# A lower part made by an adding transfer in the second product of an MLP

## The chip, the cores and the metric

The kernel runs on one core of a Trainium2 chip, as one program. The metric is the device time of one execution in microseconds; the number given for a kernel is the median of its runs. A core has five engines that run side by side: TensorE (PE in the profile, its weight loads PEld), VectorE (DVE), ScalarE (ACT), GpSimd (POOL) and SyncE (SP), and 16 DMA engines that move data between HBM and the on-chip memory. Instructions of one engine start in the order in which they stand in its queue, and engines wait for each other on semaphores.

## The reference

A trunk of two layers over 256 tokens of width 2048, in float32. Layer 0 mixes tokens with a convolution module, layer 1 with multi-head latent attention. After each mixer stands an MLP with a squared ReLU, of width 8192, and at the end a norm:

```python
def sq_relu_mlp(h, w1, w2):
    return jnp.square(jax.nn.relu(h @ w1)) @ w2

for layer in range(DEPTH):
    h = rms_norm(x, norm_mixer_g[layer])
    x = x + (conv_module(h, ...) if layer % 2 == 0 else mla(h, ...))
    h = rms_norm(x, norm_mlp_g[layer])
    x = x + sq_relu_mlp(h, mlp_w1[layer], mlp_w2[layer])
return rms_norm(x, final_norm_g)
```

## The kernel before

Every float32 product is made of three matmuls on a reduced-precision type: each operand is split into an upper part `hi` (a copy to that type) and a lower part `lo` (what is left), and `mm3` adds upper by upper, lower by upper and upper by lower into one PSUM bank. The weights come from HBM as they are and are split on the chip. `load` fills a tile `raw` of 1 MB (three of them), with a transfer on SP's queue; `split_half` makes from each half of it a `hi` on ACT (line 159) and a `lo` on DVE (line 160). `hi` and `lo` tiles have six buffers each (`WB`), 128 partitions by 1024 columns.

An MLP is done in two halves of its 8192 hidden columns (`HALVES`). In each half, `mlp` first makes the hidden activations (lines 514 and 515) and splits them into `gh`, `gl` or, for a third of them, into seven combined blocks `sh`, `sl`. Then `down` multiplies them by the second weight matrix. It goes over two column blocks of 1024 output columns (`n2`), and in each over 16 pairs of 128 rows of the weights (`NPAIR`). So there are 2 layers x 2 halves x 2 blocks = 8 passes over 16 pairs.

Pairs 0, 3, 6, 9 and 12 are done with seven block products in place of eight (`seven`): DVE adds weight blocks into a tile `T` (lines 449, 453 and 455), `split_part` splits the blocks and their sums into four `hi` and four `lo` tiles (lines 389 and 390), and PE makes 7 x 3 = 21 matmuls. After pair 12, `early` takes the four banks that are complete and adds their combinations to the residual `xs`: copies on ACT (lines 431 and 432), two subtractions on DVE (433 and 434), two on POOL (437 and 438), and additions to `xs` on DVE (line 555).

The other 11 pairs of a pass are ordinary: two `hi` and two `lo` tiles, and 2 x 2 x 2 x 3 = 24 matmuls (two token tiles `t`, two column blocks of 512, two halves `k`) by `plain`. In the very last pass (layer 1, second half, second block; `last`), pairs 13, 14 and 15 are kept, and their matmuls are done output by output at the end, so that the final norm of each token tile can begin early.

In the MLP no order is written out by hand: a scheduler places the instructions of each engine from the order of the program, its dependences and its own costs. In the convolution and the attention the order is that of the program.

Of the kernel before, what the change touches and what calls it, by code (L numbers as in the profile page):

```python
# [10 lines left out]
F32 = mybir.dt.float32  # L11
F32R = mybir.dt.float32r
BF16 = mybir.dt.bfloat16
I32 = mybir.dt.int32
AF = mybir.ActivationFunctionType
ALU = mybir.AluOpType
AX = mybir.AxisListType

P = 128
D = 2048  # L20
KC = D // P
T = 2
S = T * P
FF = 4 * D
NB = 512
# [16 lines left out]
WB = 6  # L42
# [34 lines left out]
def trunk_kernel(  # L77
# [26 lines left out]
    nc = tc.nc  # L104
# [4 lines left out]
    wpool = ctx.enter_context(tc.tile_pool(name="wpool", bufs=2))  # L109
# [23 lines left out]
    def nm(s):  # L133
        uid[0] += 1
        return f"{s}_{uid[0]}"


    def acc_tile():
        return psum["acc"].tile([P, NB], F32, tag="acc", name=nm("acc"))
# [4 lines left out]
    def load(srcs, nj):  # L144

        raw = wpool.tile([P, nj, sum(src.shape[-1] for src in srcs)], F32, tag="raw", name=nm("raw"), bufs=3)
        at = 0
        for src in srcs:
            nc.sync.dma_start(raw[:, :, at : at + src.shape[-1]], src)
            at += src.shape[-1]  # L150
        return raw

    def split_half(raw, h, eng):

        _, nj, cols = raw.shape
        js = slice(h * nj // 2, (h + 1) * nj // 2)
        hi = wpool.tile([P, nj // 2, cols], F32R, tag="hi", name=nm("hi"), bufs=WB)
        lo = wpool.tile([P, nj // 2, cols], F32R, tag="lo", name=nm("lo"), bufs=WB)
        nc.scalar.activation(hi, raw[:, js, :], AF.Copy)  # L159
        eng.tensor_tensor(lo, raw[:, js, :], hi.bitcast(F32), op=ALU.subtract)  # L160
        return hi, lo

    def split(raw, eng):
# [13 lines left out]
    def rows(w, k0, nk, c0, n):  # L177

        return w[k0 * P : (k0 + nk) * P, c0 : c0 + n].rearrange(
            "(j p) n -> p j n", p=P  # L180
        )

    def mm3(ps, sh, sl, mh, ml, start, stop):

        nc.tensor.matmul(ps, sh, mh, start=start, stop=False)  # L185
        nc.tensor.matmul(ps, sl, mh, start=False, stop=False)  # L186
        nc.tensor.matmul(ps, sh, ml, start=False, stop=stop)  # L187
# [196 lines left out]
    def split_part(src, eng):  # L384

        _, nj, cols = src.shape
        hi = wpool.tile([P, nj, cols], F32R, tag="hi", name=nm("hi"), bufs=WB)
        lo = wpool.tile([P, nj, cols], F32R, tag="lo", name=nm("lo"), bufs=WB)
        nc.scalar.activation(hi, src, AF.Copy)  # L389
        eng.tensor_tensor(lo, src, hi.bitcast(F32), op=ALU.subtract)  # L390
        return hi, lo

    NPAIR = FF // P // HALVES // 2
# [12 lines left out]
    def down(w, k_lo, hs, xs_add, prepare, pre, mp, finish=None, before=None):  # L406

        for n2 in range(NNB // 2):
            na, nb = 2 * n2, 2 * n2 + 1
            banks, seen = {}, set()  # L410
            outs = {(1, nb): "P2", (1, na): "Q3", (0, nb): "P4", (0, na): "Q0"}

            def mm(name, sh, sl, mh, ml, stop):
                if name not in banks:
                    banks[name] = acc_tile()
                mm3(banks[name], sh, sl, mh, ml, name not in seen, stop)
                seen.add(name)

            def plain(p, parts, n, t):
                for k in range(2):  # L420
                    wh, wl = parts[k]
                    gh, gl = (a[:, k, t * P : (t + 1) * P] for a in hs[p])
                    bs = slice((n - na) * NB, (n - na + 1) * NB)
                    mm(outs[t, n], gh, gl, wh[:, 0, bs], wl[:, 0, bs], p == NPAIR - 1 and k == 1)

            def early():

                s1, s5 = (mp.tile([P, NB], F32, tag="v", name=nm("v"), bufs=2) for _ in range(2))
                uv = mp.tile([P, 2, NB], F32, tag="W", name=nm("W"), bufs=1)
                u, v = uv[:, 0, :], uv[:, 1, :]  # L430
                nc.scalar.activation(s1, banks["P1"], AF.Copy)
                nc.scalar.activation(s5, banks["Q5"], AF.Copy)
                nc.vector.tensor_tensor(u, s1, banks["Q6"], op=ALU.subtract)
                nc.vector.tensor_tensor(v, u, banks["Q7"], op=ALU.subtract)
                xs_add(nb, s1, 1)
                xs_add(nb, v, 0)
                nc.gpsimd.tensor_tensor(u, s5, u, op=ALU.subtract)
                nc.gpsimd.tensor_tensor(v, s5, v, op=ALU.subtract)
                xs_add(na, u, 1)
                xs_add(na, v, 0)  # L440

            last = finish is not None and n2 == NNB // 2 - 1
            kept = []
            for p in range(NPAIR):
                raw = load([rows(w, k_lo + 2 * p, 2, na * NB, 2 * NB)], 2)
                if seven(p):
                    x = raw.rearrange("p j (b n) -> p (j b) n", b=2)
                    tt = mp.tile([P, 4, NB], F32, tag="T", name=nm("T"), bufs=1)
                    nc.vector.tensor_tensor(  # L449
                        tt[:, 0:2, :], x[:, 0:1, :].broadcast_to([P, 2, NB]), x[:, 1:3, :], op=ALU.add  # L450
                    )
                    one = split_part(x[:, 1:2, :], nc.vector)
                    nc.vector.tensor_tensor(tt[:, 2, :], tt[:, 0, :], x[:, 2, :], op=ALU.add)
                    t13 = split_part(tt[:, 0:2, :], nc.vector)
                    nc.vector.tensor_tensor(tt[:, 3, :], tt[:, 2, :], x[:, 3, :], op=ALU.add)
                    t24 = split_part(tt[:, 2:4, :], nc.vector)
                    two = split_part(x[:, 2:4, :], nc.vector)
                    gh, gl = hs[p]
                    for name, f, part, i in (
                        ("P1", A11, one, 0), ("Q5", S1, t13, 0), ("Q7", S3, t13, 1), ("Q6", S2, t24, 0),  # L460
                        ("P4", A22, t24, 1), ("P2", A12, two, 1), ("Q3", S4, two, 0),
                    ):
                        mm(name, gh[:, f, :], gl[:, f, :], part[0][:, i, :], part[1][:, i, :],
                           p == LAST_SEVEN and name in ("P1", "Q5", "Q6", "Q7"))
                    if p == LAST_SEVEN:
                        early()
                else:
                    parts = [split_half(raw, h, nc.vector) for h in range(2)]
                    if last and p > LAST_SEVEN:
                        kept.append((p, parts))  # L470
                    else:
                        for t in range(T):
                            for n in (na, nb):
                                plain(p, parts, n, t)
                    if p > LAST_SEVEN and pre:
                        prepare(pre.pop(0))
            if last:
                before()
                for t in range(T):
                    for n in (nb, na):  # L480
                        for p, parts in kept:
                            plain(p, parts, n, t)
                        xs_add(n, banks[outs[t, n]], t)
                        prepare(n, t)
                    finish(t)
            else:
                for t, n in ((0, nb), (1, nb), (1, na), (0, na)):
                    xs_add(n, banks[outs[t, n]], t)
                pre += [na, nb]
        if finish is None:  # L490
            while pre:
                prepare(pre.pop(0))
# [74 lines left out]
    with ExitStack() as cx:  # L567
# [14 lines left out]
        sh = cv.tile([P, KC, S], F32R, name="sh")  # L582
# [203 lines left out]
        with tc.manual_schedule():  # L786
# [6 lines left out]
            for h in range(2):  # L793
                hs = slice(h * D // 2, (h + 1) * D // 2)
# [49 lines left out]
            for c in range(1, KC + 1):  # L844
                n = UC * c
# [84 lines left out]
            for m in range(NP):  # L930
# [4 lines left out]
                for j in range(2):  # L935
                    k = 2 * m + j
                    wh, wl = conv_w(NU + m, j)
                    for b in range(2):
                        bs = slice(b * NB, (b + 1) * NB)
# [7 lines left out]
                t, i = divmod(m, NNB)  # L947
                sl = slice(i * NB, (i + 1) * NB)
# [67 lines left out]
    with ExitStack() as cx:  # L1016
        at = cx.enter_context(tc.tile_pool(name="at", bufs=1, reuse_waits="tile"))
# [56 lines left out]
        raws, parts = {}, {}  # L1074
# [263 lines left out]
        with tc.manual_schedule():  # L1338
# [8 lines left out]
            ps = [[acc_tile() for _ in range(2)] for _ in range(T)]  # L1347
            for k in range(KC):
                u, j = divmod(k, 2)
# [4 lines left out]
                wh, wl = w_at(("kv", u), j)  # L1354
# [9 lines left out]
            ps = [acc_tile() for _ in range(T)]  # L1364
            for k in range(KC):
                u, j = divmod(k, 4)
# [3 lines left out]
                wh, wl = w_at(("q", u), j)  # L1370
# [55 lines left out]
            for g in range(NG):  # L1426
                for i in range(HG):
                    h = g * HG + i

                    n = -(-len(work) // (HG - i))  # L1430
# [116 lines left out]
```

## Time and profile before

| | us |
|---|---|
| median of 3 runs (lowest to highest) | 1974.55 (1972.83 to 1974.62) |
| the profiled execution | 1974.39 |
| its span, first to last instruction | 1972.6 |
| DMA queue of SP: 363.63 MB | 58.1% of 16 engines |

The page names a group of instructions by its line in the kernel, its engine, and the tiles that it writes and reads (`lo<-raw,hi`). "L160 DVE" is so the subtraction of `split_half` on DVE. A timeline row has the start and the length in us, then the engine, line and operation, and in brackets the idle time of the engine before it with what ended it. The length of a matmul is modelled and overlaps the next one, so the pace of PE is read from the distance of the starts. A windows row gives for a stretch its length, the busy time of PE, PEld, DVE, ACT and POOL with the number of their instructions, the granted clock of PE, the busy share of the DMA engines and GB/s.

### The profile page before, as it was taken

The page shows a single profiled execution, that of the slowest core. Times are in us where ns is not written, and L with a number is a line of the kernel's source. Part 1 is how long each engine was busy: PE and PEld are TensorE (multiplying, and loading weights), DVE is VectorE, ACT ScalarE, POOL GpSimd, SP SyncE. Part 2 cuts the span into 40 slices and gives each one's busy share as a digit, 9 for nine tenths or more (in the row PEclk, how much of TensorE's full clock was granted, in tenths as well). Part 3 has the DMA queues.
Part 4 walks back from the last instruction along what each step waited for, and adds up shares of the span by engine and source line. Part 5 has one row for each costly group of instructions (what it writes and reads, how often), then busy time and mean ns, then how long its engine had stood idle before and what let it go on. Part 6 is the DMA issues. An engine that isn't in the chain of part 4 may idle for free.

```text
span 1972.6 us, 28263 instructions
## 1 busy us (share of the span) xinstructions
PE 1945.4 (99%) x10940; PEld 1708.3 (87%) x10940; DVE 1410.4 (71%) x2043; ACT 1032.7 (52%) x1481; POOL 311.0 (16%) x260
## 2 busy tenths in 40 slices
PE   7999999999999999999999999999999999999997
PEld 7999888888888888888899998888888888888886
DVE  5999866666787766678776666566677776667786
ACT  5456655444544444455466665544454444445453
POOL 5999300010000101000001310010100001010000
PEclk9999999999999999999999999999999999999999
DMA  8666456655656665565655445566556676565563
GB/s 241 179 185 186 135 192 186 188 188 168 204 198 203 220 188 188 168 206 195 207 168 179 121 150 178 183 187 188 189 178 200 200 226 188 187 189 199 198 203 117
DMA packets 210502, 367.60 MB, mean 186 GB/s; under 512 B 15416, under 2 KB 89792, under 8 KB 210112
## 3 DMA queue, kind: packets, MB, share of 16 engines
q1 hardware_dynamic: 209344, 363.63, 58.1%
q10 hardware_dynamic: 1024, 2.17, 0.3%
q8 instruction: 85, 1.39, 0.3%
q14 instruction: 49, 0.40, 0.1%
HBM read 363.68 MB, written 2.10 MB: 185 GB/s over the span
## 4 chain that ended last, share of the span: by engine, by line
PE 89%; DVE 8%; ACT 1%; DMA 1%; issue 0%; POOL 0%; POOLq 0%; DVEq 0%; ACTq 0%
PE acc L514 24%; PE acc L187 15%; PE acc L186 15%; PE acc L185 15%; PE acc L515 12%; DVE sum L721 6%; PE acc L620 1%; PE acc L621 1%; PE acc L619 1%; PE acc L241 1%; DVE lo L160 1%; PE sum L669 0%; ACT hi L159 0%; PE acc L1317 0%; DMA xs<-in_x 0%
## 5 line engine op out<-in xcount | busy, mean ns | idle before, releaser
L160 DVE TENSOR_TENSOR lo<-raw,hi 128x1024 fp32r<-128x1024 f32 (+1 forms) x550 | 651.4, 1207 | 367.7 <-ACT hi L159 360.9
L159 ACT ACTIVATE hi<-raw 128x1024 fp32r<-128x1024 f32 (+2 forms) x616 | 622.5, 1040 | 432.4 <-PE acc L514 227.4
L514 PE MATMUL acc<-xt,hi 128*128 128x512 f32 x2048 | 710.5, 390 | 0.0
L515 PE MATMUL acc<-xt,lo 128*128 128x256 f32 x2048 | 578.4, 282 | 0.0
L514 PEld LDWEIGHTS acc<-xt,hi 128*128 128x128 f32 x2048 | 384.4, 188 | 79.7
L515 PEld LDWEIGHTS acc<-xt,lo 128*128 128x128 f32 x2048 | 388.0, 189 | 0.1
L187 PE MATMUL acc<-lo,gh 128*128 128x512 f32 x704 | 274.9, 391 | 2.0 <-DVE lo L160 2.0
L185 PE MATMUL acc<-hi,gh 128*128 128x512 f32 x704 | 274.8, 390 | 0.0
L186 PE MATMUL acc<-hi,gl 128*128 128x512 f32 x704 | 274.7, 390 | 0.0
L389 ACT ACTIVATE hi<-T 128x1024 fp32r<-128x1024 f32 x80 | 84.9, 1062 | 161.9 <-DVE T L449 72.6
L721 DVE SCALAR_TENSOR_TENSOR sum<-ub,w_dw,sum 128x256 f32<-128x256 f32 x400 | 163.7, 503 | 7.1 <-ACT sum L677 6.0
L160 POOL TENSOR_TENSOR lo<-raw,hi 128x1024 fp32r<-128x1024 f32 x66 | 157.5, 2407 | 23.9 <-ACT hi L159 23.9
L529 POOL TENSOR_TENSOR W<-W 128x256 f32<-128x256 f32 x20 | 31.9, 1598 | 819.9 <-DVE W L525 693.9
L185 PE MATMUL acc<-hi,sh 128*128 128x512 f32 x408 | 159.6, 391 | 0.0
L187 PE MATMUL acc<-lo,sh 128*128 128x512 f32 x408 | 159.0, 390 | 0.0
L187 PEld LDWEIGHTS acc<-lo,gh 128*128 128x128 f32 x704 | 132.8, 189 | 30.0 <-DVE lo L160 2.5
L186 PEld LDWEIGHTS acc<-hi,gl 128*128 128x128 f32 x704 | 132.5, 188 | 27.7
L185 PEld LDWEIGHTS acc<-hi,gh 128*128 128x128 f32 x704 | 132.5, 188 | 27.2
L619 PE MATMUL acc<-xt,hi 128*128 128x256 f32 x512 | 144.6, 282 | 0.0
L620 PE MATMUL acc<-xt,hi 128*128 128x256 f32 x512 | 143.2, 280 | 0.5 <-DVE xt L198 0.5
L621 PE MATMUL acc<-xt,lo 128*128 128x256 f32 x512 | 143.2, 280 | 0.3 <-POOL lo L160 0.3
L390 DVE TENSOR_TENSOR lo<-T,hi 128x1024 fp32r<-128x1024 f32 x80 | 97.9, 1225 | 51.6 <-ACT hi L389 51.3
(264 smaller groups left out, 2655.3 us busy)
## 6 DMA issues: line engine op xcount, KB each, us to landing
raw<-in_mlp_w SPq DMA_DIRECT2D x256, 1024.0 KB, 5.5
raw<-in_conv_w_pw SPq DMA_DIRECT2D x64, 512.0 KB, 5.1
raw<-in_conv_w_pw SPq DMA_DIRECT2D x16, 1024.0 KB, 5.0
raw<-in_mla_w_o SPq DMA_DIRECT2D x16, 1024.0 KB, 5.5
raw<-in_mla_w_kv_up SPq DMA_DIRECT2D x8, 1024.0 KB, 5.5
raw<-in_mla_w_in SPq DMA_DIRECT2D x8, 576.0 KB, 3.7
raw<-in_mla_w_in SPq DMA_DIRECT2D x4, 1024.0 KB, 7.1
raw<-in_mla_w_q_up SPq DMA_DIRECT2D x16, 256.0 KB, 3.6
```

What stands on the lines that cost most here:

```text
L159: nc.scalar.activation(hi, raw[:, js, :], AF.Copy)
L160: eng.tensor_tensor(lo, raw[:, js, :], hi.bitcast(F32), op=ALU.subtract)
L185: nc.tensor.matmul(ps, sh, mh, start=start, stop=False)
L186: nc.tensor.matmul(ps, sl, mh, start=False, stop=False)
L187: nc.tensor.matmul(ps, sh, ml, start=False, stop=stop)
L390: eng.tensor_tensor(lo, src, hi.bitcast(F32), op=ALU.subtract)
L514: nc.tensor.matmul(ps[b], wh[:, bs], xhl(k), start=k == 0, stop=False)
L515: nc.tensor.matmul(ps[b][:, :S], wl[:, bs], xh(k), start=False, stop=k == KC - 1)
L619: nc.tensor.matmul(o, wh[:, bs], xh(k), start=k == 0, stop=False)
L620: nc.tensor.matmul(o, wh[:, bs], xl(k), start=False, stop=False)
L621: nc.tensor.matmul(o, wl[:, bs], xh(k), start=False, stop=k == KC - 1)
L721: nc.vector.scalar_tensor_tensor(out=out, in0=ubs[c][:, w : w + S], scalar=tap(c, w), in1=pcs[c], op0=ALU.mult, op1=ALU.add)
```

## The change

In ordinary pairs the first half is split as before. For the second half, `split_dma` makes the upper part on ACT, then on ACT the negative of the upper part into the `lo` tile, and then issues a transfer on POOL's queue that reads the same weights (512 KB) from HBM a second time and adds them onto the `lo` tile. The subtraction of that half on DVE is gone.

The order of the matmuls in ordinary pairs changes too: `whole` takes for each half first the eight matmuls with the upper part of the weights, then the four with the lower part. The pairs that are kept in the very last pass still go through `plain`.

```diff
+    def split_dma(raw, j, src):
+
+        hi = wpool.tile([P, 1, raw.shape[2]], F32R, tag="hi", name=nm("hi"), bufs=WB)
+        lo = wpool.tile([P, 1, raw.shape[2]], F32R, tag="lo", name=nm("lo"), bufs=WB)
+        nc.scalar.activation(hi, raw[:, j : j + 1, :], AF.Copy)
+        nc.scalar.activation(lo, hi.bitcast(F32), AF.Copy, scale=-1.0)
+        nc.gpsimd.dma_start(lo[:, 0, :], src, accum_op=ALU.add)
+        return hi, lo
...
+            def whole(p, parts):
+
+                at = [(t, n, slice((n - na) * NB, (n - na + 1) * NB)) for t in range(T) for n in (na, nb)]
+                for k in range(2):
+                    wh, wl = parts[k]
+                    gh, gl = ([a[:, k, t * P : (t + 1) * P] for t in range(T)] for a in hs[p])
+                    for t, n, bs in at:
+                        ps = bank(outs[t, n])
+                        nc.tensor.matmul(ps, gh[t], wh[:, 0, bs], start=first(outs[t, n]), stop=False)
+                        nc.tensor.matmul(ps, gl[t], wh[:, 0, bs], start=False, stop=False)
+                    for t, n, bs in at:
+                        stop = p == NPAIR - 1 and k == 1
+                        nc.tensor.matmul(bank(outs[t, n]), gh[t], wl[:, 0, bs], start=False, stop=stop)
...
-                    parts = [split_half(raw, h, nc.vector) for h in range(2)]
+                    parts = [
+                        split_half(raw, 0, nc.vector),
+                        split_dma(raw, 1, w[(k_lo + 2 * p + 1) * P : (k_lo + 2 * p + 2) * P, na * NB : (na + 2) * NB]),
+                    ]
                     if last and p > LAST_SEVEN:
                         kept.append((p, parts))
                     else:
-                        for t in range(T):
-                            for n in (na, nb):
-                                plain(p, parts, n, t)
+                        whole(p, parts)
```

More of the change, by code (lines that the diff above doesn't have):

```diff
@@ L411, in down, with bank, first, mm @@
             outs = {(1, nb): "P2", (1, na): "Q3", (0, nb): "P4", (0, na): "Q0"}
-            def mm(name, sh, sl, mh, ml, stop):
+            def bank(name):
                 if name not in banks:
                     banks[name] = acc_tile()
-                mm3(banks[name], sh, sl, mh, ml, name not in seen, stop)
+                return banks[name]
+            def first(name):
+                new = name not in seen
                 seen.add(name)
+                return new
+            def mm(name, sh, sl, mh, ml, stop):
+                mm3(bank(name), sh, sl, mh, ml, first(name), stop)
             def plain(p, parts, n, t):
```

## The prediction

> **What bounds the kernel now.** I read the page's busy table first, then windows of one period of the second product, then its timeline, then the end.
>
> ```profile
> PE   1945.4 (99%) x10940; PEld 1708.3 (87%) x10940; DVE 1410.4 (71%) x2043; ACT 1032.7 (52%) x1481; POOL 311.0 (16%) x260
> 600.60:616.30 15.70, 15.70 (x71) 13.00 (x70) 11.33 (x12) 7.78 (x9) 0.00 (x0) 1.00 0.61 200
> 616.30:632.00 15.70, 15.70 (x71) 12.99 (x70) 11.22 (x12) 7.67 (x9) 0.00 (x0) 1.00 0.62 205
> ```
>
> The two window rows give, after the stretch: its length, then PE, PEld, DVE, ACT and POOL with their counts, the granted clock, the DMA engines' busy share and GB/s. PE is busy for all of the 15.70 us; DVE for some 11.3, ACT 7.7. In this product PE is the bound and DVE is cover.
>
> How fast PE goes is read from the starts in its timeline:
>
> ```profile
> 614.05 0.39 PE L185 MATMUL acc<-hi,gh 128*128 128x512 f32 x1
> 614.28 0.39 PE L186 MATMUL acc<-hi,gl 128*128 128x512 f32 x1
> ...
> 624.71 0.39 PE L187 MATMUL acc<-lo,gh 128*128 128x512 f32 x1
> 624.93 0.39 PE L185 MATMUL acc<-hi,sh 128*128 128x512 f32 x1
> ...
> 629.69 0.39 PE L185 MATMUL acc<-hi,gh 128*128 128x512 f32 x1
> ```
>
> An ordinary pair reads gh and gl, a seven-product pair sh and sl. One period (two ordinary pairs, one of seven products) is 629.69 - 614.05 = 15.64 us for 24 + 24 + 21 = 69 matmuls: 0.2267 us each, with nothing lost between them. So a pair takes 5.44 us or 4.76 us (21 matmuls, 624.93 to 629.69). There is nothing to win here unless a matmul gets quicker.
>
> The one place with a wait is the very end, the last column block of layer 1, where pairs 13 to 15 are kept and run by output:
>
> ```profile
> 1943.18 0.39 PE L185 MATMUL acc<-hi,gh 128*128 128x512 f32 x1
> 1948.40 0.39 PE L185 MATMUL acc<-hi,gh 128*128 128x512 f32 x1
> 1950.82 0.50 PE L187 MATMUL acc<-lo,gh 128*128 128x512 f32 x1 [2.04 <-DVE lo L160]
> 1953.30 0.63 PE L186 MATMUL acc<-hi,gl 128*128 128x512 f32 x1
> 1944.35 2.13 POOL L437 TENSOR_TENSOR W<-v,W 128x512 f32<-128x512 f32 x1 [79.13 <-DVE W L434]
> 1947.12 1.73 POOL L438 TENSOR_TENSOR W<-v,W 128x512 f32<-128x512 f32 x1 [0.63 <-DVE xs L555]
> 1949.55 2.35 DVE L160 TENSOR_TENSOR lo<-raw,hi 128x1024 fp32r<-128x1024 f32 x2
> 1951.60:1955.10 3.50, 3.50 (x10) 2.70 (x9) 1.05 (x2) 0.72 (x2) 0.00 (x0) 0.51 0.00 0
> ```
>
> Pair 15's lower parts stand on DVE behind residual adds that need POOL's L438. PE loses 1950.82 - 1948.40 - 0.23 = 2.2 us, and then runs 3.5 us at a granted clock of 0.51, which costs 1.7 us more. So 3.9 us are all that the change could return here.
>
> **The change, part by part.** There are 11 ordinary pairs in each of 8 column blocks (2 layers, 2 halves, 2 blocks): 88. The prices:
>
> ```profile
> L160 DVE TENSOR_TENSOR lo<-raw,hi 128x1024 fp32r<-128x1024 f32 x526 | 633.3, 1227 | 358.1 <-ACT hi L159 351.7 <-PE acc L241 5.1
> L159 ACT ACTIVATE hi<-raw 128x1024 fp32r<-128x1024 f32 x592 | 606.7, 1055 | 420.5 <-PE acc L514 227.4 <-issue 92.5 <-PE acc L186 78.9
> 624.27 3.90 ACT L159 ACTIVATE hi<-raw 128x1024 fp32r<-128x1024 f32 x4 [3.43 <-issue]
> 625.37 4.63 DVE L160 TENSOR_TENSOR lo<-raw,hi 128x1024 fp32r<-128x1024 f32 x4 [3.08 <-ACT hi L159]
> q1 hardware_dynamic: 209344, 363.63, 58.1%
> raw<-in_mlp_w SPq DMA_DIRECT2D x256, 1024.0 KB, 5.5
> raw<-in_conv_w_pw SPq DMA_DIRECT2D x64, 512.0 KB, 5.1
> raw<-in_mla_w_q_up SPq DMA_DIRECT2D x16, 128.0 KB, 2.4
> ```
>
> Removed: 88 subtractions on DVE, 88 x 1.227 = 108 us of work, 2.45 us in a period. Off the path: gain 0.
>
> Added: 88 negating copies on ACT, 88 x 1.055 = 93 us. ACT goes from 7.7 to 9.8 us of 15.64. They stand between the two upper copies of a pair and what follows on ACT's queue. Price 0, covered by ACT's idle 5.8 us; without that cover 1.055 us a pair.
>
> PE order: still 24 matmuls in a pair, 12 on the half that DVE makes, then 8 uppers of the other, then its 4 lowers. So the late lower part is first read at matmul 20, 20 x 0.2267 = 4.53 us into the pair. Price 0 at an unchanged pace. Freed earlier: the raw half is read by one engine only, and the first half's tiles come free in mid-pair. Both only help the loads.
>
> The new chain: negating copy on ACT, issue on POOL, 512 KB from HBM added onto the tile. The tight case is the pair after a seven-product one. With six hi and six lo buffers, and four of each taken by the seven products, its second lower tile reuses that of the ordinary pair just before them. In the old trace this is seen at 624.27: ACT starts the pair's upper copies when PE is at the end of that pair (624.71), and the pair itself starts at 629.69. In the new order the negating copy may start as soon as that pair's last lower matmul has read the tile, 0.2 us after the pair's end by its 0.39 us, and ends 1.05 us later: 1.3 us. PE needs the sum 4.76 + 4.53 = 9.29 us after the pair's end. **Left for issue and transfer: 8.0 us.** The second ordinary pair reuses the seven products' second tile, which comes free some 2.5 us before they end (after 9 of 21 matmuls); with one upper copy more in its chain its slack is some 2.3 us more.
>
> What issue and transfer cost, no row shows. From below: 2.4 us, the 128 KB load. From above: two 512 KB landings in a row, for reading the old contents and for the load, plus 2.4 us on POOL: 12.6 us. I take 5.1 us for the load and 1.9 us for POOL (its L437 and L438 took 2.13 and 1.73): 7.0 us, nearest to the one row of this size. It fits under 8.0 with 1.0 us to spare, so price 0 in the periods.
>
> POOL's queue: in the blocks' middle only these transfers. At pair 12 the two subtractions of `early` stand between the transfers of pairs 13, 14 and 15. In seven blocks pair 14's sum is needed 10 us after pair 12's end, and a transfer issued at L437's end, 3.3 us after it, lands at 10.3 by my price: 0 to 0.3 us each, 2 us in all at most, taken as 0. In the last block the order by output asks for it much earlier. There the built order puts 22 matmuls before pair 14's late part: needed at 1943.18 + 22 x 0.2267 = 1948.2. It is issued after L437, at 1944.35 + 2.13 = 1946.5, and lands at 1953.5. L438 follows at about 1948.4, ends at 1950.1, and only then is pair 15's issued: 1957.1, needed nine matmuls after 1953.5, at 1955.5 or later. That is the 32nd matmul of the stretch; in the trace before the 32nd starts at 1953.30, with 0.9 us of half clock still to pay. So +3.8 us, less 0.9, and up to 1.7 for a clock that falls again: +2.9 to +4.6, with a quick transfer (4 us) nearer 0. I take +3.6.
>
> SP's queue keeps its loads; 88 x 0.5 MB = 46 MB join 364 MB. The share of 0.615 in a period is 9.6 us for 3 MB, 3.2 us a MB; 1 MB more at the plain price makes 12.8 us of 15.64. Covered.
>
> **Sum.** The profiled execution took 1974.39 us (span 1972.6), 0.16 under the median 1974.55. 1974.39 + 3.6 = **1978.0 us**. Less than 0.2%, 4 us, can't be told from no change here.
>
> **A rule against the change.** The window's DMA share is 0.62 with plain loads. The Trainium skill (Collectives: The Full Stack, "The bandwidth ceiling: the fold count and why AG ≠ RS ≠ AR") says that a reduction by DMA reads two sources for each chunk on the same ring, and so delivers half the rate of a copy. By it the period's DMA work would be 9.6 + 6.4 = 16.0 us and the sum about 1996 us. No row of before shows an adding transfer.
>
> **The rivals.**
>
> *The chain is longer than 8.0 us.* Then PE waits in every pair that follows a seven-product one, 5 in a block, 40 in all, for the excess. POOL may be slow to issue while DVE works:
>
> ```profile
> L529 POOL TENSOR_TENSOR W<-W 128x256 f32<-128x256 f32 x20 | 31.9, 1598 | 819.9 <-DVE W L525 693.9 <-ACT v L521 126.0
> L697 POOL TENSOR_TENSOR tp<-tp,tp 128x256 f32<-128x256 f32 x23 | 16.8, 737 | 0.2
> ```
>
> POOL's work on one shape took 737 or 1598 ns, and DVE runs four subtractions in a row for 4.63 us. Half of that, 2.3 us, on top of 7.0 plus what loads in flight add: 9.5 us, 1.5 us over, 60 us in all: 2038 us. At the upper bound of 12.6 us it is 184 us and, where each stop halves the clock, up to 40 x 1.7 = 68 more: 2226 us. For it: the slack is one microsecond on a price that no row shows. Against: the issue is one instruction and needs no data. Chance 0.30. The Trainium skill (SBUF — State Buffer, "SBUF: two separate sides") says that some DVE operations lock POOL out, so that it cannot write the descriptors of its transfers; no run here shows it yet.
>
> *The DMA engines become the bound.* To add, a transfer must read the old contents too: up to twice the work of a plain one. At double price a period lasts 16.0 us, 0.4 us more, 44 periods: +18, about 1996 us with the end. At three times the price, 19.2 us, +158: 2136 us. It decides from a price of 1.9 plain ones. For: a period of loads already reached 0.75 (below). Against: loads have slack, ACT waits for PE's buffers and not for them. Chance 0.18, most of it near 2000.
>
> ```profile
> 585.00:600.60 15.60, 15.60 (x70) 12.92 (x70) 13.36 (x15) 8.12 (x9) 0.00 (x0) 1.00 0.75 248
> ```
>
> *Faster.* In the new lower passes two matmuls in a row share their stationary operand, 4 of 24. A 256-column matmul goes every 0.117 us:
>
> ```profile
> 99.95 0.28 PE L620 MATMUL acc<-xt,hi 128*128 128x256 f32 x1
> 100.06 0.28 PE L621 MATMUL acc<-xt,lo 128*128 128x256 f32 x1
> ```
>
> so of 0.2267 us about 2 x 0.117 - 0.227 = 0.007 us is not columns. Saved on 352 matmuls that is 2.5 us; on all 2112, 15 us: 1963 us. It decides from 1.9 ns a matmul. Against: PEld and PE count the same, so loads aren't left out. The end's 3.9 us could also vanish, if a transfer took under 1.7 us, below the 2.4 us of 128 KB. Chance 0.05.
>
> **How the numbers follow.** Hidden but for the end: 0.42 (+0 to +5 us, some 0.25 of it inside 0.2%); chain too long 0.30; DMA-bound 0.18; faster 0.05; 0.05 for what I don't see, half of it near no change. The likeliest gives 1978, its own range 1973 to 1980. The range 1973 to 2085 takes in all of that, the chain up to 2.6 us over (0.23) and DMA up to 2.5 prices (0.15): 0.8. Slower by over 0.2%: 0.30 + 0.18 + 0.17 + 0.02 = 0.67; same 0.25 + 0.03 = 0.28; faster 0.05.
>
> **What would show it.** Right: PE fully busy in the windows of a period, 0.2267 us a matmul, DVE near 9 us and ACT near 10 us of 15.64, DMA share near 0.8, and a longer wait for the late lower part only after 1943. Wrong: idle time of PE before the late lower matmuls in each period, released by the transfer (chain), loads that land late and ACT waiting for them (DMA), a granted clock under 1.00 in mid-block, or matmul starts off 0.227 us. What would make me wrong above all is the unshown price of the adding transfer.

## The result and the profile after

The changed kernel takes 2029.26 us (median of 4 runs, 2025.99 to 2033.14) against 1974.59 us before. The ratio is 1.0278, with a 95% interval of 1.0257 to 1.0299: 54.7 us slower. The prediction was 1978.0 us with a range of 1973 to 2085, and 0.67 for slower. The direction and the range held. The point did not: the case called the likeliest, a hidden transfer, is not what happened. What happened is the first rival, the chain that is longer than its slack (2038 us).

The profiled execution of the changed kernel is the longest of the four, 2033.14 us; its span is 2031.4. The first fence has lines of its page: the busy table, the DMA queues, the chain of work that ended last, and two groups and the transfers' own line. The second has the chain's line of the kernel before.

```profile
PE 1962.4 (97%) x10940; PEld 1707.3 (84%) x10940; DVE 1325.9 (65%) x1955; ACT 1124.1 (55%) x1569; POOL 386.2 (19%) x348
q1 hardware_dynamic: 209344, 363.63, 57.0%
q0 software_dynamic: 12672, 46.14, 12.0%
PE 64%; DMA 17%; DVE 9%; issue 5%; ACT 4%; POOL 1%; POOLq 0%; DVEq 0%; ACTq 0%
L454 PE MATMUL acc<-lo,gh 128*128 128x512 f32 x680 | 187.9, 399 | 40.2 <-DMA lo<-in_mlp_w 36.1
L169 POOL DMA_DIRECT2D lo<-in_mlp_w x88 | 76.8, 872 | 622.5 <-ACT lo L168 534.8
lo<-in_mlp_w POOLq DMA_DIRECT2D x88, 512.0 KB, 8.4
```

```profile
PE 89%; DVE 8%; ACT 1%; DMA 1%; issue 0%; POOL 0%; POOLq 0%; DVEq 0%; ACTq 0%
```

DVE lost 84 us of work (the prediction counted 108) and ACT gained 91 (93), and both are still far from busy. DMA, 1% of the chain before, is 17% of it now: PE waits for the adding transfer. The chain counts a transfer's whole length; PE's own row has 40.2 us of idle time, 36.1 of them put down to the transfer. The transfer lands 8.4 us after the start of its issue (median of 88), where the prediction had 7.0 in all. Per megabyte it costs the engines 0.120 x 2031.4 / 46.14 = 5.28 us, a plain load 0.570 x 2031.4 / 363.63 = 3.18 us.

How one wait looks is seen in three timelines of the changed kernel, of ACT, of POOL and of PE, around a pair that follows a seven-product one (pair 7). The ordinary pair before ended at 1509.37, where the first matmul with `sh` starts:

```profile
1508.72 1.06 ACT L167 ACTIVATE hi<-raw 128x1024 fp32r<-128x1024 f32 x1 [1.72 <-PE acc L451]
1509.81 1.06 ACT L168 ACTIVATE lo<-hi 128x1024 fp32r<-128x1024 f32 x1
```

```profile
1511.27 0.86 POOL L169 DMA_DIRECT2D lo<-in_mlp_w  x1 [12.48 <-ACT lo L168]
```

```profile
1509.37 0.39 PE L194 MATMUL acc<-hi,sh 128*128 128x512 f32 x1
1518.43 0.39 PE L451 MATMUL acc<-hi,gl 128*128 128x512 f32 x1
1519.38 0.69 PE L454 MATMUL acc<-lo,gh 128*128 128x512 f32 x2 [0.56 <-DMA lo<-in_mlp_w]
```

The negating copy ends at 1510.87. PE would read the sum one matmul after 1518.43, at 1518.66: 7.8 us of slack, where the prediction worked out 8.0. (The copy starts 0.44 us after the pair's end and not 0.2, because the upper copy, which waits for an upper tile, stands before it.) PE starts at 1519.38, 0.72 us late. So issue and transfer took 8.5 us from the copy's end: 0.40 until POOL issues, and 8.1 from there until PE has the sum.

In windows of a period, to be read as those of before, PE is no longer busy throughout:

```profile
1494.50:1511.00 16.50, 16.30 (x73) 13.19 (x72) 9.07 (x9) 9.95 (x12) 1.73 (x2) 1.00 0.90 252
1511.00:1527.40 16.40, 15.84 (x70) 12.84 (x69) 8.98 (x9) 9.65 (x11) 1.72 (x2) 1.00 0.94 258
```

DVE has 9.0 us of work in 16.4, ACT 9.8, and the DMA engines are busy for 0.90 to 0.94 of the time.

Where the waits stand is found by going through the starts of PE: where a late lower matmul starts more than 0.228 us after the matmul before it, PE waited. The table goes by the place of the pair in its block, with the waits summed over the 8 blocks. Slack is the time from the end of the negating copy to the start at which PE would read the sum if it came in time; the three kept pairs of the last block count in the waits and the landings, not in the slack:

| pair | what it follows | slack, median us | issue to landing, median us | wait, us |
|---|---|---|---|---|
| 1 | seven products, start of a block | 7.1 | 7.8 | 9.4 |
| 2 | an ordinary pair, start of a block | 9.9 | 10.0 | 8.0 |
| 4, 7, 10, 13 | seven products | 7.8 to 8.0 | 7.7 to 8.0 | 19.6 |
| 5, 8, 11 | an ordinary pair | 10.8 to 11.0 | 8.9 to 9.3 | 1.2 |
| 14 | an ordinary pair, behind `early` on POOL | 9.3 | 9.2 | 12.9 |
| 15 | an ordinary pair | 14.5 | 9.9 | 0.5 |

Beside the landing a chain holds 0.40 us from the copy's end to the issue (1.41 in pair 14) and 0.14 from the landing to PE's start. So pairs 4, 7, 10 and 13 need some 8.4 us for a slack of 7.8.

The waits add up to 51.6 us. Before, PE waited 2.2 us for a lower part, in the last block. All starts of PE together lost some 57 us more than before against their usual distance, of 58.8 us by which the spans of the profiled executions differ. Most of the rest is clock: three stretches of 3.4 us at half clock ahead of the last 10 us, against one before.

### The profile page after: what moved, and what is told of

Same layout as the page of the kernel before. It is cut to its first block, busy times and chain, and to the rows that moved or that the text cites. A ratio compares the mean times of both kernels' runs of the same rounds, so it can differ in the third digit from the quotient of the medians.

```text
span 2031.4 us, 28533 instructions
## 1 busy us (share of the span) xinstructions
PE 1962.4 (97%) x10940; PEld 1707.3 (84%) x10940; DVE 1325.9 (65%) x1955; ACT 1124.1 (55%) x1569; POOL 386.2 (19%) x348
## 3 DMA queue, kind: packets, MB, share of 16 engines
q1 hardware_dynamic: 209344, 363.63, 57.0%
q0 software_dynamic: 12672, 46.14, 12.0%
q8 instruction: 86, 1.41, 0.3%
## 4 chain that ended last, share of the span: by engine, by line
PE 64%; DMA 17%; DVE 9%; issue 5%; ACT 4%; POOL 1%; POOLq 0%; DVEq 0%; ACTq 0%
PE acc L545 22%; DMA lo<-in_mlp_w 15%; PE acc L546 12%; DVE sum L752 6%; PE acc L196 5%; PE acc L194 5%; PE acc L195 5%; PE acc L454 3%; PE acc L451 2%; PE acc L450 2%; ACT hi L167 1%; ACT hi L159 1%; ACT lo L168 1%; DMA raw<-in_mlp_w 1%; PE acc L651 1%
## 5 line engine op out<-in xcount | busy, mean ns | idle before, releaser
L160 DVE TENSOR_TENSOR lo<-raw,hi 128x1024 fp32r<-128x1024 f32 (+1 forms) x462 | 556.6, 1211 | 364.9 <-ACT hi L159 341.6
L159 ACT ACTIVATE hi<-raw 128x1024 fp32r<-128x1024 f32 (+2 forms) x528 | 542.5, 1039 | 428.7 <-PE acc L545 229.2
L450 PE MATMUL acc<-hi,gh 128*128 128x512 f32 x680 | 266.8, 392 | 0.0
L451 PE MATMUL acc<-hi,gl 128*128 128x512 f32 x680 | 266.4, 392 | 0.0
L454 PE MATMUL acc<-lo,gh 128*128 128x512 f32 x680 | 187.9, 399 | 40.2 <-DMA lo<-in_mlp_w 36.1
L169 POOL DMA_DIRECT2D lo<-in_mlp_w x88 | 76.8, 872 | 622.5 <-ACT lo L168 534.8
L454 PEld LDWEIGHTS acc<-lo,gh 128*128 128x128 f32 x680 | 125.0, 189 | 82.0 <-issue 33.6
L167 ACT ACTIVATE hi<-raw 128x1024 fp32r<-128x1024 f32 x88 | 92.7, 1054 | 68.1 <-PE acc L451 62.2
```

Source lines behind the costliest of these rows:

```text
L450: nc.tensor.matmul(ps, gh[t], wh[:, 0, bs], start=first(outs[t, n]), stop=False)
L451: nc.tensor.matmul(ps, gl[t], wh[:, 0, bs], start=False, stop=False)
L454: nc.tensor.matmul(bank(outs[t, n]), gh[t], wl[:, 0, bs], start=False, stop=stop)
```

## The experiments

In the text the kernel with the change is the changed kernel; each experiment is told as a diff against it, if nothing else is said. In the diffs `w[...]` stands for the slice of the weights that the change spells out.

**The order alone.**

```diff
                     parts = [
                         split_half(raw, 0, nc.vector),
-                        split_dma(raw, 1, w[...]),
+                        split_half(raw, 1, nc.vector),
                     ]
```

> New matmul order in ordinary pairs, both lower parts made on DVE as before, no adding transfer. Theory (the time goes into waiting for the transfer): no wait is left, 1972 to 1977 us, PE starts 0.227 us apart. Rival of the prediction, a faster pace from the shared stationary operand: under 1970.6 us. A third possibility, that the order itself costs: above 1985 us.

It took 1975.08 us (10 runs), ratio 1.0002 with an interval of 0.9992 to 1.0011. The starts of PE in these pairs are as far apart as before, 0.2266 us in the mean. So the new order costs nothing, and the shared stationary operand brings nothing. This rules out the rival in which a matmul gets quicker.

**The transfer alone.**

```diff
-                        whole(p, parts)
+                        for t in range(T):
+                            for n in (na, nb):
+                                plain(p, parts, n, t)
```

> Adding transfer kept, old matmul order: the late lower part is then read first at matmul 6 of a pair and not at matmul 20, 14 x 0.2267 = 3.2 us earlier. Theory (chain longer than its slack): every pair after a seven-product one waits some 3 us, 40 x 3.1 = 125, pair 14 another 1.5 us in 8 blocks, and a granted clock that falls after the longer waits: 2090 to 2190 us. Rival (the DMA engines are the bound, the same bytes move): 2020 to 2040 us as in the changed kernel.

It took 2260.96 us, ratio 1.1449 (1.1432 to 1.1466). The same bytes move, so a bound by the DMA engines would have left the time where it was. The theory had the sign, and a size that was too low (2090 to 2190 us). Its costliest group of waits:

```profile
L196 PE MATMUL acc<-lo,gh 128*128 128x512 f32 x704 | 318.0, 453 | 186.7 <-DMA lo<-in_mlp_w 186.7
```

And a window of its trace, right behind such a wait:

```profile
551.80:558.60 6.80, 5.87 (x14) 4.65 (x15) 0.00 (x0) 0.80 (x1) 0.00 (x0) 0.50 0.65 169
```

By the starts of PE, the pairs that follow seven products wait 4.7 us each (183 us for the 39 that are not kept), 4.0 us more than in the changed kernel. The expectation has the late part read at the sixth matmul; in the built order it is the tenth in 34 of the 39, 11 x 0.2267 = 2.5 us earlier than the 21st. Another 1.7 us are on ACT. The lines are around pair 4 of the first block, whose preceding pair ended at 541.06:

```profile
540.35 1.06 ACT L159 ACTIVATE hi<-raw 128x1024 fp32r<-128x1024 f32 x1 [3.53 <-PE acc L195]
542.27 1.04 ACT L159 ACTIVATE hi<-raw 128x1024 fp32r<-128x1024 f32 x1
543.21 1.04 ACT L168 ACTIVATE lo<-hi 128x1024 fp32r<-128x1024 f32 x1
```

```profile
545.82 0.39 PE L194 MATMUL acc<-hi,gh 128*128 128x512 f32 x1
552.73 0.77 PE L196 MATMUL acc<-lo,gh 128*128 128x512 f32 x1 [4.71 <-DMA lo<-in_mlp_w]
```

In the old order both upper tiles are in use until the pair's end, so the upper copies start late, and an upper copy of the next pair stands before the negating one: it ends 3.2 us after the pair's end, 1.5 in the changed kernel. Of the 286 us some 190 are waits. The rest fits the clock: in the window PE was granted 0.50, and there are 42 stretches with a lowered clock in this execution (4 in the changed kernel; both counts have one at the very end), 235 us in all. The waits of 4.7 us cost about half as much again.

**No adding.**

```diff
-        nc.gpsimd.dma_start(lo[:, 0, :], src, accum_op=ALU.add)
+        nc.gpsimd.dma_start(lo[:, 0, :], src)
```

> As the changed kernel, but the transfer on POOL's queue overwrites the lower tile and adds nothing (the lower part of the second half is then the weights themselves, so the product is another one); same bytes from HBM, same queue, same waits. Theory that adding makes the transfer long: landing falls from 8.4 to some 6.5 us, nearly all waits go, 1974 to 1985 us. Rival that issue, HBM and the loads beside it make it long: landing stays above 7.5 us and the time above 2010 us.

It took 1992.71 us, ratio 1.0090 (1.0075 to 1.0105). Lines of its page:

```profile
q0 software_dynamic: 12672, 46.14, 7.2%
L169 POOL DMA_DIRECT2D lo<-in_mlp_w x88 | 47.5, 540 | 607.8 <-ACT lo L168 524.7
lo<-in_mlp_w POOLq DMA_DIRECT2D x88, 512.0 KB, 6.4
```

Without the addition the transfer lands 2.0 us earlier, POOL issues it in 0.54 us and not in 0.87, and the engines' work falls to 0.072 x 1990.7 / 46.14 = 3.11 us a megabyte, that of a plain load. So adding costs 1.7 times a copy here. The waits of pairs 1, 4, 7, 10 and 13 are gone (29.0 to 0.6 us). But the time stayed above the expected 1985: pair 14 still waits 10.2 us and pair 2 8.1. Those two do not come from the adding alone. Pair 2's are all in the four blocks that open a half of an MLP, where the slack is 6.8 to 8.2 us and the plain copy takes 8.8 to 9.7.

**The transfer only where there is more slack.**

```diff
-                        split_dma(raw, 1, w[...]),
+                        split_dma(raw, 1, w[...])
+                        if p in (5, 8, 11) else split_half(raw, 1, nc.vector),
```

> The transfer is used only in pairs 5, 8 and 11 of each block (24 of the 88), whose chain had 2.3 us more slack; the other ordinary pairs make both lower parts on DVE. Theory (each transfer costs only what it misses its slack by): these pairs waited 1.2 us in all, so 1973 to 1978 us. Rival (each transfer costs its share, by DMA work or by disturbing loads): 24/88 of 54.7 = 15 us, 1987 to 1992 us.

It took 1980.36 us, ratio 1.0031 (1.0019 to 1.0044), nearer to the theory than to the rival but above its range. PE's wait for the transfer is small:

```profile
L454 PE MATMUL acc<-lo,gh 128*128 128x512 f32 x680 | 182.7, 390 | 2.7 <-DMA lo<-in_mlp_w 2.7
lo<-in_mlp_w POOLq DMA_DIRECT2D x24, 512.0 KB, 9.8
```

By the starts of PE these 24 transfers made PE wait 3.7 us, all in pair 11, where the landing reached 11.2 us against a slack of 10.6. Some 2 us of the 5.9 are not traced to a place. The landing is also of use: here no two adding transfers are in flight at once, and still they take 9.8 us, so the loads beside one are enough to make it long.

**Issued earlier.** With six buffers, the second tile that an ordinary pair after seven products takes is the second of the ordinary pair before. If the half with the transfer takes its tiles first, they are those of the half that is done at matmul 12.

```diff
-                    parts = [
-                        split_half(raw, 0, nc.vector),
-                        split_dma(raw, 1, w[...]),
-                    ]
+                    src = w[...]
+                    late = split_dma(raw, 1, src) if p % 3 == 1 else None
+                    parts = [split_half(raw, 0, nc.vector)]
+                    parts.append(late or split_dma(raw, 1, src))
```

> As the changed kernel, same transfers, but in the pairs after seven products (1, 4, 7, 10, 13) the tiles of the half with the transfer are taken first. They then reuse the tiles of the earlier half of the ordinary pair before, free at its matmul 12 and not at its end, so that the issue comes some 2.6 us earlier. Theory (slack of 8.0 us against a landing of 7.8): the waits of these pairs, 27 us, go, pair 14's grow by some 4: 2000 to 2012 us, landing unchanged. Rival (the DMA engines are full): no change, 2025 to 2033 us.

It took 2016.93 us (four runs, three near 2017 and one of 2006.06), ratio 1.0200 (1.0177 to 1.0222): 12 us less than the changed kernel, where 17 to 29 were expected. The negating copy of pairs 4, 7, 10 and 13 ends 2.8 us earlier, and the waits of pairs 1, 4, 7, 10 and 13 are gone, 29.0 to 0.0 us, with the same bytes and the same adding. This is the clearest sign that these waits are a matter of slack. What was not foreseen is how much would come back: pair 14's waits grew from 12.9 to 18.1 us and pair 2's from 8.0 to 12.2, and the clock was lowered more often (9 stretches against 4). One of pair 14's:

```profile
1547.53 0.39 PE L451 MATMUL acc<-hi,gl 128*128 128x512 f32 x1
1551.06 1.32 PE L454 MATMUL acc<-lo,gh 128*128 128x512 f32 x3 [3.15 <-DMA lo<-in_mlp_w]
```

**POOL's queue cleared.**

```diff
-                nc.gpsimd.tensor_tensor(u, s5, u, op=ALU.subtract)
-                nc.gpsimd.tensor_tensor(v, s5, v, op=ALU.subtract)
+                nc.vector.tensor_tensor(u, s5, u, op=ALU.subtract)
+                nc.vector.tensor_tensor(v, s5, v, op=ALU.subtract)
```

> As the changed kernel, but the two subtractions of early that stand between the transfers of pairs 13, 14 and 15 on POOL's queue are done on DVE. Theory (pair 14's transfer is issued 2.8 us late behind the first of them): its waits, 12.9 us, go, and with them a fall of the clock: 2011 to 2019 us. Rival (pair 14's transfer is long because of the loads beside it, 9.2 us): no change, 2025 to 2033 us.

In the changed kernel POOL's timeline at pairs 13, 14 and 15 shows the transfer of pair 14 right behind the subtraction of `early`, 5.8 us after that of pair 13 (an ordinary second pair is issued 3.0 us after the first). ACT's row is the negating copy of pair 14:

```profile
1544.13 0.88 POOL L169 DMA_DIRECT2D lo<-in_mlp_w  x1 [12.53 <-ACT lo L168]
1547.74 2.21 POOL L467 TENSOR_TENSOR W<-v,W 128x512 f32<-128x512 f32 x1 [2.73 <-DVE W L464]
1549.89 0.88 POOL L169 DMA_DIRECT2D lo<-in_mlp_w  x1
1550.59 1.71 POOL L468 TENSOR_TENSOR W<-v,W 128x512 f32<-128x512 f32 x1
1552.25 0.87 POOL L169 DMA_DIRECT2D lo<-in_mlp_w  x1
```

```profile
1547.43 1.05 ACT L168 ACTIVATE lo<-hi 128x1024 fp32r<-128x1024 f32 x1
```

The copy ends at 1548.48 and the issue starts at 1549.89, 1.41 us later, where 0.40 is usual. So POOL's subtraction holds the issue up by 1.0 us, not by 2.8 as the expectation has it; the other 1.8 are on ACT, where the two copies of `early` and an upper copy of pair 15 go first.

The run took 2020.59 us, ratio 1.0231 (1.0217 to 1.0245). Pair 14's waits fell by 8.5 us, from 12.9 to 4.4, and the time by 8.7. The issue now starts 0.40 us after the copy in all 8 blocks, and 8 x 1.0 is 8.1 us. So two thirds of these waits are POOL's queue. The rest is a shorter slack: the landing (8.8 us) is no longer than in pairs 5, 8 and 11 (9.2 to 9.6), but the copy of pair 14 ends 9.2 us before its read and theirs 10.7 to 10.9.

**Both.**

> Both of these together. Theory: left are the waits of pair 2 at the start of a block, 8 us, a fall of the clock there, and what the end costs: 1982 to 1995 us, still not under the kernel before.

It took 1998.19 us, ratio 1.0111 (1.0095 to 1.0126), 3 us above the range. Left are 13.1 us of pair 2 and 7.3 of pair 14, and five stretches of a lowered clock.

**The kernel before, without its wait at the end.** The same two lines, in the kernel before.

> The kernel before, with the two subtractions of early on DVE in place of POOL. Theory (in the last block PE waits 2.2 us for lower parts that stand on DVE behind POOL's subtraction, and loses 1.7 us to the clock): 1970.5 to 1973 us. Rival (two more operations on DVE cost as much): 1973.5 to 1977 us.

It took 1970.64 us (11 runs) against 1974.53, ratio 0.9982 (0.9973 to 0.9991). The wait of 2.2 us in the last block and the clock that fell after it are gone: the whole 3.9 us that the prediction gave as the most that could be had there. It needs nothing of the change, and of the kernels run it has the lowest median. Its DVE timeline has both subtractions in 0.69 us each where POOL took 2.13 and 1.73:

```profile
1945.99 0.69 DVE L437 TENSOR_TENSOR W<-v,W 128x512 f32<-128x512 f32 x1
1946.60 0.69 DVE L438 TENSOR_TENSOR W<-v,W 128x512 f32<-128x512 f32 x1
```

**Only transfers that are covered.** Against the run with both edits:

```diff
                     src = w[...]
-                    late = split_dma(raw, 1, src) if p % 3 == 1 else None
+                    plain_split = p in (2, 14) or last and p > LAST_SEVEN
+                    late = split_dma(raw, 1, src) if p % 3 == 1 and not plain_split else None
                     parts = [split_half(raw, 0, nc.vector)]
-                    parts.append(late or split_dma(raw, 1, src))
+                    if plain_split:
+                        parts.append(split_half(raw, 1, nc.vector))
+                    else:
+                        parts.append(late or split_dma(raw, 1, src))
```

> As the run with both edits (tiles of the late half first in pairs after seven products, the subtractions of early on DVE), but pairs 2 and 14 of each block and the pairs kept at the very end make both lower parts on DVE. 71 of the 88 transfers are left. Theory (a transfer costs only what it misses its slack by, and the clock that falls after it): hardly a wait is left, 1970.5 to 1977 us, between the kernel before and the same with early on DVE. Rival (transfers cost something each, beside their waits): 71/88 of the excess, 1990 us or more.

Left are 70 transfers (the expectation says 71). It took 1972.93 us (10 runs), ratio to the kernel before 0.9995 (0.9985 to 1.0005). Lines of its page, of the groups and the DMA issues:

```profile
L454 PE MATMUL acc<-lo,gh 128*128 128x512 f32 x680 | 182.1, 390 | 0.8 <-DMA lo<-in_mlp_w 0.7
lo<-in_mlp_w POOLq DMA_DIRECT2D x70, 512.0 KB, 8.2
```

And a window in mid-block:

```profile
1478.00:1494.00 16.00, 16.00 (x72) 13.25 (x71) 9.35 (x10) 10.82 (x11) 1.72 (x2) 1.00 1.00 288
```

Four fifths of the transfers, nearly as long as before (8.2 us), cost 2.3 us beside the kernel before with the same edit of `early` (the two were run in different series), and nothing beside the kernel before. PE's starts show some 1.5 us of waits for them. So a transfer costs little but what it misses its slack by, and the clock after it. The window shows PE busy for all of 16.00 us with the DMA engines at 1.00: a DMA share near one is here no bound by itself.

## Why the prediction was right or wrong

**The bound, right.** PE is what limits the product and DVE was cover: the order alone measured 1.0002, and the kernel with 70 covered transfers, in which DVE has fewer subtractions as well, is no faster than the one without them and the same edit of `early`.

**The slack, right, but for pair 1.** 8.0 us were worked out from the pace and the buffers, 7.8 to 8.0 are seen in pairs 4, 7, 10 and 13. Pair 1, which the prediction counted with them, has 7.1 in the median and 4.3 in one block. That the slack is tight in the pairs after seven products and wider in the others is what the table of waits and the run with the tiles taken first show.

**The price of issue and transfer, wrong: the step that failed.** It was a guess of 7.0 us between 2.4 and 12.6, set against 8.0. From the copy's end to PE's start it is some 8.4 us in the tight pairs: 0.40 before the issue, 7.8 or a little more to the landing, 0.14 behind it. The two terms of the 7.0 were both off. POOL's issue, put at 1.9 us, is 0.87. The transfer, put at 5.1, takes some 7 us and more. In the last block, where no load is in flight, issue to landing is 5.8 us, though two adding transfers overlap there; with loads beside it and no second adding transfer it was 9.8. So the loads add 2 to 4 us, for which the 7.0 had nothing, and the addition some 2 (8.4 us against 6.4). An excess of 0.7 us, over 40 pairs, is 29.0 us in place of 0. With a step that repeats 40 times, a microsecond to spare on an unknown price was little ground to call the hidden case the likeliest.

**POOL's queue, named and then set to nothing.** "Lands at 10.3 by my price: 0 to 0.3 us each, 2 us in all at most" became 12.9 us. With 9.2 us for pair 14's landing in place of 7.0 the same sum gives 3.3 + 9.2 = 12.5 against 10, less the 0.5 that pair 13's wait gives back: 2.0 us in each of seven blocks, 14, where 11.3 are seen in them. The mechanism was right for two thirds of it, as the run with POOL's queue cleared shows, and the term was mis-sized by the same price; that ACT's copies make this pair's slack shorter was not foreseen.

**Not foreseen: pair 2** at the start of each block, 8 us. Its landing is long, 10.0 us, but that is not all: 7.0 of the 8.0 us lie in the four blocks that open a half of an MLP, where its slack is 8.3 to 9.9 us, against 10.0 to 11.4 in the other four. There ACT still has copies of the hidden activations before the negating one. The prediction gave all second pairs some 10.3.

**The end**, predicted at +2.9 to +4.6: in the changed kernel PE waits 1.9, 1.6 and 0.5 us there, 4.0 in place of 2.2 us, and the clock stays at 1.00. By that it is +1.8 less the 1.7 us of clock that before lost, nothing. With no load in flight the transfers were quicker there (5.8 us) than the 7.0 assumed: the one price was too low in mid-block and too high at the end.

**The rivals.** "The chain is longer than 8.0 us" is what happened, at an excess of 0.7 and not 1.5 us. That its 2038 us lies so near to 2029 is luck: the pairs it speaks of wait 29.0 us and not 60, and 20.9 more come from pairs 2 and 14, for which it had nothing. The range held because it took in this rival. The reason given for it, that POOL is held up by DVE, is not borne out: of the 88 issues 60 ran wholly beside a busy DVE, at a mean of 0.873 us, and the other 28 took 0.870. So the rule of the Trainium skill (SBUF — State Buffer, "SBUF: two separate sides"), that some DVE operations lock POOL out, shows no effect on the issues here.

"The DMA engines become the bound" fell: the same 46 MB took 2017, 2029 and 2261 us, by where their sums were needed, and 37 MB of them 1973 us. The price of an adding transfer, 1.7 plain ones, is also under the 1.9 from which that rival would decide. The rule named for it (the Trainium skill, Collectives: The Full Stack, "The bandwidth ceiling: the fold count and why AG ≠ RS ≠ AR"), half the rate for a reduction by DMA, is stated there for rings between cores. The trace agrees with its direction: the engines' work per megabyte is 1.7 times that of a copy, not twice.

## What to carry to other kernels

Before work is moved from a covered engine to another resource, write down the chain that replaces it, from the release of its buffer to the read of its result, and set its length beside the slack at its tightest place; if the price is unknown and the place repeats, a small margin is no reason to call the fit the likeliest case. Use the resource where the slack is wide: 70 of the 88 transfers cost some 2 us in all once the others were left out. Take the length of a transfer from a stretch with as many loads in flight as there will be, not from one alone. And look first at the waits that are there: two subtractions moved from POOL to DVE gave 3.9 us, the change none.

## What was unexpected of the hardware

An adding transfer of 512 KB landed 5.8 us after its issue with no load beside it and 7.7 to 10 us with loads beside it; over all pairs it took 8.4 us (median), and 6.4 if it only copied. POOL's issue took 0.87 us for an adding transfer and 0.54 for a copy, and in the changed kernel the same beside a busy DVE as without one. The DMA engines were busy at a share of 1.00 for 16 us without a wait on PE.

Waits of 2 to 5 us of PE were often followed by a stretch of 3.4 us at half clock, but their length alone does not decide it. In the changed kernel a wait of 2.0 us was followed by one and two waits of 2.2 us were not; without the adding, a wait of 3.4 us was not either, as these lines of PE and of the window behind it show (clock 1.00):

```profile
1820.14 0.39 PE L451 MATMUL acc<-hi,gl 128*128 128x512 f32 x1
1823.81 0.70 PE L454 MATMUL acc<-lo,gh 128*128 128x512 f32 x2 [3.28 <-DMA lo<-in_mlp_w]
```

```profile
1823.80:1829.80 6.00, 5.99 (x27) 4.98 (x28) 3.41 (x4) 3.59 (x4) 0.53 (x1) 1.00 0.88 292
```

What else decides, no run here shows.
